# A hybrid linear-attention and pooling layer: a norm product in its own tile, context gates by pairs of heads, key weights in other tiles

## The chip, the cores and the metric

One core of a Trainium2 chip runs the whole program. The metric is device time in microseconds (us) of one execution. The engines are named as the profile names them: PE (TensorE, matrix products), DVE (VectorE), ACT (ScalarE), POOL (GpSimd) and SP (SyncE, which issues the transfers).

## The reference

One layer of a diffusion backbone works on 1024 latent tokens and 256 context tokens of width 1024. All is float32. Cut to what matters here:

```python
h  = rmsnorm(x, norm_g) * (1 + scale) + shift            # context and latent alike
q, k, v, la_f, la_b, zA, uB, zB, gA, gB = mixer_inputs(h, w_in, ...)
gk = lowrank @ w_up + b                                  # rank 16, per direction
la = log_sigmoid(gk) / 16                                # log decay, 4 heads x 128 keys
...
S_t = diag(a_t) S_(t-1) + k_t v_t^T ;  o_t = q_t S_t      # both directions
# the latent scan starts from the context's final state of the same direction
...
merged = sigmoid(gA) * yA + sigmoid(gB) * yB
x_new  = x + gate_x * (merged @ w_out)
out    = x_new * rsqrt(mean(x_new ** 2) + eps) * final_norm_g
```

Of the context, only the final state of each head and direction is needed: keys times the decay that is still to come, transposed, times values.

## The kernel before, in words

Every float32 operand of a product is split in two: ACT copies it to a rounded `hi` tile and DVE subtracts that to get a `lo` tile (`split`, L84). A product is then three matmuls: hi by hi, hi by lo, lo by hi. Helpers record nearly all instructions, so most rows carry a helper's line: L64 is any ACT operation, L67 a DVE operation of two tensors, L71 and L72 a DVE operation with a scalar, L79 a matmul, L330 the scan.

Tiles come from pools by tag. Each tag has a fixed number of buffers (L38): `wr` 2 (raw weights as loaded), `wh` and `wl` 4 each (their split), `s2` 8, `on` 1, `bx` 1, `z` 2. A new tile of a tag waits until the oldest one's last reader is done. The eight PSUM banks of 128x512 are tags too (L40): `pj` 3, `sc` 2, `o`, `st` and `tr` one each. The order of the instructions on each engine is not the order of the program's text: a scheduler places them, and weight loads with their splits are placed ahead (`tc.high_priority` in `wslot`, L259) once the first context head is done (L697).

The program has these stages around the change:

1. Norms and modulation, and the first projections with all the input weights that come first.
2. **Context gates** (`ctx_gates`, L336). For each of four heads and two directions, `gate_in` (L323) makes a 128x256 result with two matmuls of 64 rows (the low-rank factor by the up-projection's hi and lo). One head's two directions share the bank of tag `o`. ACT takes the absolute value out of the bank (with the bias) and DVE the minimum with zero. When all heads are there, ACT does Exp, then Ln, each over two heads at a time, in the tiles `z`; DVE subtracts and scans (L330) along the tokens. The rest of the decays is computed from the scans.
3. **Latent gates of head 0** (`gates`, L462): the same in banks `sc`, `sc`, `o` and `tr`, with 128x512 results, and Exp and Ln over one `bx` tile of 128x2048.
4. **Context states** (`ctx_state`, called in the loop at L698): for heads 1 to 3 the key weights (`weights_k`, L383, through `wslot`: one load into `wr`, two pairs of `wh`/`wl`) and value weights (`weights_v`: two loads, four pairs). `ctx_k` makes 24 matmuls into a `pj` bank, `ctx_v` two times 24. `ctx_state` multiplies the keys by two exponentials, transposes them on PE into bank `tr`, copies them to the one `on` tile on ACT, and multiplies them with the values into bank `st` (8 matmuls).
5. The latent attention of four heads, the pooling branch, the branches' projections.
6. **The output product**, in seven block products (`out_product`, L1227) whose results are added to the residual tiles `y` (these have the tile names `h`, `kt`, `sw`, `v`, `S`) by DVE (`add_y`, L1198). Products 5 and 6 complete eight token tiles of 128 rows, four each: 12 matmuls per tile into one bank. `finish` (L1209) then squares the completed half on ACT (with the row sum), multiplies it by the final gain `fg` on DVE in place (both in `square`, L1201), makes the scale of the row (a DVE operation on 128x1, a POOL power), scales one half on DVE and the other on ACT, and stores both halves (256 KB each). The other half of a tile has been squared and multiplied before (`first_done`).

Of the kernel before, what the change touches and what calls it, by code (L numbers as in the profile page):

```python
# [10 lines left out]
F32R = mybir.dt.float32r  # L11
# [4 lines left out]
P = 128  # L16
# [27 lines left out]
def hybrid_kernel(ctx: ExitStack, tc: tile.TileContext, x, ctx_in, rows, w_mod, b_gate_row,  # L44
# [213 lines left out]

    def wslot(src, shape, col_scale=None):  # L259

# [3 lines left out]
        with tc.high_priority() if ahead[0] else nullcontext():  # L264
# [4 lines left out]
            for k0 in range(0, nk, per):  # L269
                kn = min(per, nk - k0)  # L270
                hi, lo = T("wh", [P, kn, n], F32R), T("wl", [P, kn, n], F32R)
                split(hi, lo, raw[:, k0:k0 + kn, :])
                parts += [(hi[:, i, :], lo[:, i, :]) for i in range(kn)]
        return parts

    def wcols(w, c0, n=P):
        return w[:, c0:c0 + n].rearrange("(k p) n -> p k n", p=P)
# [58 lines left out]
    def ctx_gates():  # L336
# [3 lines left out]
        for h in range(NH):  # L340
            pt = PT("o")
            for d in range(2):
                pd = pt[:, d * LC:(d + 1) * LC]
                bcol = gate_in(pd, h, d, 0, LC)
                act(e[h // 2][:, h % 2, d, :], pd, AF.Abs, bias=bcol)
                ts(xm[h // 2][:, h % 2, d, :], pd, bcol, ALU.add, 0.0, ALU.min)
# [35 lines left out]

    def weights_k(h):  # L383
        return wslot(wcols(w_in, O_K + h * P), [P, KT, P])

# [312 lines left out]
    for h in range(1, NH):  # L698
        ctx_state(h, ctx_k(weights_k(h)), ctx_v(weights_v(h)))
    o_dram = [dr.tile([KT, P, 256], F32, name=f"o{h}") for h in range(NH)]  # L700
# [508 lines left out]
    def finish(t, dh):  # L1209
        square(t, dh)  # L1210
        ts(yst[:, t, 1:2], yss[:, t, dh:dh + 1], 1.0 / D, ALU.mult, yst[:, t, 0:1], ALU.add)
        nc.gpsimd.tensor_tensor(out=yst[:, t, 2:3], in0=yst[:, t, 1:2], in1=mhalf, op=ALU.pow)
        for dh in range(2):
            if dh:
                act(y[t][dh], y[t][dh], scale=yst[:, t, 2:3])
            else:
                ts(y[t][dh], y[t][dh], yst[:, t, 2:3], ALU.mult)
            load(out[t * P:(t + 1) * P, dh * HALF:(dh + 1) * HALF], y[t][dh])

# [35 lines left out]
    for t in range(CPH):  # L1255
        add_y(CPH + t, 1, sums[t])
        first_done(CPH + t, 1)
    out_product(5, others, True)
    for t in range(CPH):
        add_y(CPH + t, 0, others[t])  # L1260
        finish(CPH + t, 0)
    out_product(6, sums, True)
    for t in range(CPH):
        add_y(t, 1, sums[t])
        finish(t, 1)

# [64 lines left out]
```

## Time and profile before

| | us |
|---|---|
| median of 3 runs (range) | 1116.48 (1116.02 to 1117.79) |
| the profiled execution's own time | 1116.68 |
| its span in the profile | 1114.9 |
| PE busy | 1080.9 (97%) |
| DVE busy | 819.7 (74%) |
| ACT busy | 511.4 (46%) |
| granted clock of PE, mean | 0.996 |

The span counts from the first to the last instruction of the profile; the execution's own time is 1.8 us longer. Busy time is what instructions took, so that a share near 100% over the whole program says which engine sets the time on the mean, and the stages where the share is lower must be looked at one by one. The granted clock is a share of the full 2.4 GHz.

### The profile page before, as it was taken

How to read it: one execution, taken by the hardware profiler on the slowest of the kernel's cores; microseconds unless marked ns; L12 is line 12 of the kernel's file. 1: busy time of each engine (PE TensorE's matmuls, PEld its weight loads, DVE VectorE, ACT ScalarE, POOL GpSimd, SP SyncE). 2: the span in 40 equal slices, each digit the busy share in tenths (PEclk: the TensorE clock that was granted, in tenths of full speed). 3: DMA queues.
4: the chain of work that ended last, by engine and by line, in shares of the span. 5: the costliest groups of instructions: out<-in, count | busy, mean ns of one | idle time of the engine just before them, and what ended most of it. 6: DMA issues, size and time to landing. Idle time of an engine off the chain costs nothing.

```text
span 1114.9 us, 16534 instructions
## 1 busy us (share of the span) xinstructions
PE 1080.9 (97%) x6073; PEld 872.6 (78%) x6073; DVE 819.7 (74%) x1518; ACT 511.4 (46%) x982; POOL 24.9 (2%) x50
## 2 busy tenths in 40 slices
PE   7999899999999999999999999999999999999995
PEld 1497887797887888888888888788887788888884
DVE  4775768487586685989989987877778786557854
ACT  4875864644644744543334343333436423124433
POOL 0000000100100000000000000000000000000001
PEclk9999999999999999999999999999999999999998
DMA  9920240310310311114331884865628658645424
GB/s 332 299 58 20 68 141 21 84 50 20 95 39 20 96 39 39 48 48 129 125 115 51 290 273 134 258 208 206 195 96 290 203 186 287 232 132 181 149 77 151
DMA packets 124470, 152.85 MB, mean 137 GB/s; under 512 B 9515, under 2 KB 77413, under 8 KB 124262
## 3 DMA queue, kind: packets, MB, share of 16 engines
q1 hardware_dynamic: 124390, 151.80, 42.8%
q8 instruction: 48, 0.79, 0.3%
q14 instruction: 32, 0.26, 0.1%
HBM read 107.72 MB, written 39.85 MB: 132 GB/s over the span
## 4 chain that ended last, share of the span: by engine, by line
PE 70%; DMA 10%; DVE 8%; ACT 6%; issue 3%; POOL 1%; SPq 0%; POOLq 0%; ACTq 0%; DVEq 0%
PE ppj L79 47%; PE psc L79 14%; PE pst L79 3%; PE po L79 2%; DMA wr<-w_in 2%; DMA h<-w_mod 2%; DVE s L67 2%; DVE wl L67 1%; PE ptr L79 1%; DMA wo_T<-t 1%; DVE wr L67 1%; ACT on L64 1%; ACT A L64 1%; ACT wh L64 1%; DMA S<-ctx 1%
## 5 line engine op out<-in xcount | busy, mean ns | idle before, releaser
L79 PE MATMUL ppj<-h,wh 128*128 128x512 f32 x730 | 238.8, 400 | 0.0
L79 PEld LDWEIGHTS ppj<-h,wh 128*128 128x128 f32 x730 | 136.1, 188 | 32.7 <-issue 3.0
L64 ACT ACTIVATE wh<-wr 128x512 fp32r<-128x512 f32 x162 | 99.6, 626 | 117.6 <-DVE wr L67 39.0
L79 PE MATMUL ppj<-h,wl 128*128 128x512 f32 x365 | 143.3, 393 | 0.0
L67 DVE TENSOR_TENSOR wl<-wr,wh 128x512 fp32r<-128x512 f32 x162 | 110.1, 688 | 35.6 <-ACT wh L64 34.7
L79 PE MATMUL ppj<-wh,h 128*128 128x256 f32 (+1 forms) x518 | 96.2, 285 | 0.0
L79 PEld LDWEIGHTS ppj<-wh,h 128*128 128x128 f32 x518 | 81.4, 192 | 1.4 <-issue 0.7
L79 PEld LDWEIGHTS ppj<-h,wl 128*128 128x128 f32 x365 | 68.6, 188 | 14.6 <-issue 1.0
L79 PE MATMUL ppj<-wl,h 128*128 128x256 f32 x259 | 73.7, 285 | 0.0
L64 ACT ACTIVATE s<-s 128x512 f32<-128x512 f32 x60 | 36.9, 628 | 30.9 <-DVE s L67 29.1
L79 PEld LDWEIGHTS ppj<-wl,h 128*128 128x128 f32 x259 | 49.7, 192 | 0.4
L75 DVE SCALAR_TENSOR_TENSOR S<-S,dec,pst 128x256 f32<-128x256 f32 x56 | 26.9, 480 | 29.4 <-PE pst L79 28.6
L64 ACT ACTIVATE s<-qk 128x256 f32<-128x256 f32 x56 | 23.5, 426 | 47.1 <-DVE qk L67 46.9
L67 DVE TENSOR_TENSOR s<-s,ppj 128x512 f32<-128x512 f32 x60 | 40.5, 681 | 1.4 <-issue 1.2
L79 PE MATMUL ppj<-S,wh 128*128 128x512 f32 (+1 forms) x124 | 38.5, 376 | 1.3 <-ACT wh L64 1.3
L79 PE MATMUL psc<-h,wh 128*128 128x512 f32 x126 | 39.2, 392 | 0.0
L64 ACT ACTIVATE qk<-wr 128x512 fp32r<-128x512 f32 x30 | 18.5, 627 | 44.2 <-DVE wr L67 26.9
L67 DVE TENSOR_TENSOR s<-s,bx 128x256 f32<-128x256 f32 (+1 forms) x64 | 30.5, 486 | 7.5 <-ACT bx L64 7.5
L79 PEld LDWEIGHTS psc<-z,s 128*64 128x64 f32 x768 | 25.0, 136 | 10.5 <-issue 9.0
L79 PE MATMUL ppj<-v,wh 128*128 128x512 f32 (+1 forms) x108 | 32.9, 367 | 0.0
L67 DVE TENSOR_TENSOR on<-wr,wr 128x512 f32<-128x512 f32 x21 | 14.5, 691 | 24.6 <-DMA wr<-w_in 18.3
L79 PE MATMUL pst<-v,kt 128*128 128x256 f32 x112 | 31.2, 395 | 1.2 <-DVE S L75 1.2
(666 smaller groups left out, 2487.8 us busy)
## 6 DMA issues: line engine op xcount, KB each, us to landing
wr<-w_in SPq DMA_DIRECT2D x65, 512.0 KB, 4.1
h<-w_mod SPq DMA_DIRECT2D x48, 256.0 KB, 5.6
qk<-sg SPq DMA_DIRECT2D x32, 256.0 KB, 5.3
sg<-s SPq DMA_DIRECT2D x28, 256.0 KB, 2.5
sw<-qk SPq DMA_DIRECT2D x64, 64.0 KB, 2.0
gb_T<-qk SPq DMA_DIRECT2D x16, 256.0 KB, 2.8
t<-w_out SPq DMA_DIRECT2D x4, 1024.0 KB, 5.5
qk<-o SPq DMA_DIRECT2D x16, 256.0 KB, 4.5
```

The costliest lines, as they stand in the source:

```text
L64: return nc.scalar.activation(out, in_, func, **kw)
L67: return nc.vector.tensor_tensor(out=out, in0=a, in1=b, op=op)
L75: return nc.vector.scalar_tensor_tensor(out=out, in0=a, scalar=s, in1=b, op0=op0, op1=op1)
L79: return nc.tensor.matmul(out, lhsT=lhsT, rhs=rhs, start=start, stop=stop, skip_group_check=joined)
```

## The change: three edits and the order they give

`wslot` takes the tags of the split tiles as an argument, and the key weights of head 1, the first of the loop at L698, use `s2` for both. `ctx_gates` takes two banks for each pair of heads, `o` for the one direction and `tr` for the other, and issues the pair's 16 matmuls before the reads. `finish` no longer calls `square`: the product with the gain goes to a new `s2` tile, the scaling and the stores are in a function `store`, and the end loops call it one tile later in the program's text. In the changed file the lines after L344 stand 2 further down, those at the end up to 8.

```diff
--- before.py
+++ after.py
@@ -256,7 +256,7 @@
 
     ahead = [False]
 
-    def wslot(src, shape, col_scale=None):
+    def wslot(src, shape, col_scale=None, tags=("wh", "wl")):
 
         _, nk, n = shape
         per = HALF // n
@@ -268,7 +268,7 @@
                 tt(raw, raw, col_scale.rearrange("p (k n) -> p k n", k=1).to_broadcast(shape), ALU.mult)
             for k0 in range(0, nk, per):
                 kn = min(per, nk - k0)
-                hi, lo = T("wh", [P, kn, n], F32R), T("wl", [P, kn, n], F32R)
+                hi, lo = [T(t, [P, kn, n], F32R) for t in tags]
                 split(hi, lo, raw[:, k0:k0 + kn, :])
                 parts += [(hi[:, i, :], lo[:, i, :]) for i in range(kn)]
         return parts
@@ -338,10 +338,12 @@
         xm = T("bx", [P, 2, 2, 2, LC])
         xm = [xm[:, i] for i in range(2)]
         for h in range(NH):
-            pt = PT("o")
+            if h % 2 == 0:
+                pts = [PT(t) for t in ("o", "tr")]
+                at = lambda h, d: pts[d][:, h % 2 * LC:(h % 2 + 1) * LC]
+                bcols = [[gate_in(at(i, d), i, d, 0, LC) for i in (h, h + 1)] for d in range(2)]
             for d in range(2):
-                pd = pt[:, d * LC:(d + 1) * LC]
-                bcol = gate_in(pd, h, d, 0, LC)
+                pd, bcol = at(h, d), bcols[d][h % 2]
                 act(e[h // 2][:, h % 2, d, :], pd, AF.Abs, bias=bcol)
                 ts(xm[h // 2][:, h % 2, d, :], pd, bcol, ALU.add, 0.0, ALU.min)
         for t in e:
@@ -380,8 +382,8 @@
             act(vc[:, t, :], proj_n(wv, hcH, hcL, slice(t * P, (t + 1) * P))[:, :256])
         return vc
 
-    def weights_k(h):
-        return wslot(wcols(w_in, O_K + h * P), [P, KT, P])
+    def weights_k(h, **kw):
+        return wslot(wcols(w_in, O_K + h * P), [P, KT, P], **kw)
 
     def weights_v(h):
         return wquad(w_in, O_V + h * 256)
@@ -696,7 +698,7 @@
     ctx_state(0, kc, ctx_v(wv))
     ahead[0] = True
     for h in range(1, NH):
-        ctx_state(h, ctx_k(weights_k(h)), ctx_v(weights_v(h)))
+        ctx_state(h, ctx_k(weights_k(h, tags=("s2", "s2") if h == 1 else ("wh", "wl"))), ctx_v(weights_v(h)))
     o_dram = [dr.tile([KT, P, 256], F32, name=f"o{h}") for h in range(NH)]
     ga_dram = [dr.tile([P, L], F32, name=f"ga{i}") for i in range(2 * NH)]
 
@@ -1207,15 +1209,19 @@
         ts(yst[:, t, 0:1], yss[:, t, dh:dh + 1], 1.0 / D, ALU.mult, EPS, ALU.add)
 
     def finish(t, dh):
-        square(t, dh)
+
+        act(T("on", [P, HALF]), y[t][dh], AF.Square, accum_out=yss[:, t, dh:dh + 1])
+        scaled = T("s2", [P, HALF])
+        tt(scaled, y[t][dh], half(fg, dh), ALU.mult)
         ts(yst[:, t, 1:2], yss[:, t, dh:dh + 1], 1.0 / D, ALU.mult, yst[:, t, 0:1], ALU.add)
         nc.gpsimd.tensor_tensor(out=yst[:, t, 2:3], in0=yst[:, t, 1:2], in1=mhalf, op=ALU.pow)
-        for dh in range(2):
-            if dh:
-                act(y[t][dh], y[t][dh], scale=yst[:, t, 2:3])
-            else:
-                ts(y[t][dh], y[t][dh], yst[:, t, 2:3], ALU.mult)
-            load(out[t * P:(t + 1) * P, dh * HALF:(dh + 1) * HALF], y[t][dh])
+
+        def store():
+            act(scaled, scaled, scale=yst[:, t, 2:3])
+            ts(y[t][1 - dh], y[t][1 - dh], yst[:, t, 2:3], ALU.mult)
+            for h_, v in ((1 - dh, y[t][1 - dh]), (dh, scaled)):
+                load(out[t * P:(t + 1) * P, h_ * HALF:(h_ + 1) * HALF], v)
+        return store
 
     def out_part(pt, i, t, g, joined):
         (a_hi, a_lo), (x_hi, x_lo) = m_ops[g][OUT_PRODUCTS[i][0]], w_ops[OUT_PRODUCTS[i][1]][g]
@@ -1255,14 +1261,16 @@
     for t in range(CPH):
         add_y(CPH + t, 1, sums[t])
         first_done(CPH + t, 1)
-    out_product(5, others, True)
-    for t in range(CPH):
-        add_y(CPH + t, 0, others[t])
-        finish(CPH + t, 0)
-    out_product(6, sums, True)
-    for t in range(CPH):
-        add_y(t, 1, sums[t])
-        finish(t, 1)
+    store = None
+    for i, t0, dh, banks in ((5, CPH, 0, others), (6, 0, 1, sums)):
+        out_product(i, banks, True)
+        for t in range(CPH):
+            add_y(t0 + t, dh, banks[t])
+            after = finish(t0 + t, dh)
+            if store:
+                store()
+            store = after
+    store()
 
 
 def shape_constants():
```

The scheduler makes a new order out of this. Outside of the stages 2 to 4 (and a few instructions of head 0's attention that were placed among them) and of the last two output products, no engine's order changes. Three places:

PE, at the end of the context gates. `po_1030` is the gate bank of a context head, `psc`, `po_1127` and `ptr_1134` the banks of the latent gates of head 0, `ppj_1181` the first product of context values:

```order
 L79 MATMUL psc_1111<-lr_1007,lr_436 128x512
-L79 MATMUL po_1030<-lr_833,lr_436 128x256
-L79 MATMUL po_1030<-lr_833,lr_437 128x256
 L79 MATMUL psc_1111<-lr_1007,lr_437 128x512
 L79 MATMUL psc_1118<-lr_1007,lr_436 128x512
 L79 MATMUL psc_1118<-lr_1007,lr_437 128x512
+L79 MATMUL ppj_1181<-wh_534,h_835 128x256
+L79 MATMUL ppj_1181<-wl_535,h_835 128x256
+L79 MATMUL po_1127<-lr_782,lr_436 128x512
+L79 MATMUL po_1127<-lr_782,lr_437 128x512
 L79 MATMUL ptr_1134<-lr_782,lr_436 128x512
 L79 MATMUL ptr_1134<-lr_782,lr_437 128x512
```

Before, the context's gate matmuls stand in eight separate pairs, some of them within the value products, and those of `po_1127` after them. Now they stand in three groups (8, 4 and 4 matmuls) ahead of the latent gates, and all latent gates stand ahead of the third value matmul.

ACT, up to `on_1349`, the copy of the transposed keys of context head 0, for which PE's state product (`pst`) waits. Before (`wh_1360` and `wh_1364` are the splits of head 1's key weights, `bx` the latent gates' Ln, `S_1286` the context values):

```order
L64 ACTIVATE wh_1360<-wr_1358 128x512
L64 ACTIVATE wh_1364<-wr_1358 128x512
L64 ACTIVATE wh_1397<-wr_1395 128x512
L64 ACTIVATE wh_1401<-wr_1395 128x512
L64 ACT_TABLE_LOAD
L64 ACTIVATE bx_1108<-bx_1108 128x2048
L64 ACTIVATE S_1286<-ppj_1313 128x256
L64 ACTIVATE on_1349<-ptr_1344 128x512
```

After (the Ln on `bx` and the splits of head 1's key weights are done ahead of these rows; `kt_1468` is head 1's exponential, `s_243` and `s_244` the latent decays):

```order
L64 ACTIVATE v_1233<-ppj_1260 128x256
L64 ACTIVATE wh_1397<-wr_1395 128x512
L64 ACTIVATE S_1286<-ppj_1287 128x256
L64 ACTIVATE wh_1401<-wr_1395 128x512
L64 ACT_TABLE_LOAD
L64 ACTIVATE kt_1468<-kt_1468 128x256
L64 ACTIVATE wh_1407<-wr_1405 128x512
L64 ACTIVATE wh_1411<-wr_1405 128x512
L64 ACTIVATE s_243_1109<-s_243_1109 128x512
L64 ACTIVATE s_244_1110<-s_244_1110 128x512
L64 ACTIVATE S_1286<-ppj_1313 128x256
L64 ACTIVATE on_1349<-ptr_1344 128x512
```

The copy to `on_1349` has moved behind splits of later weights and behind exponentials of the latent decays. On PE, the state product that waits for `on_1349` stood behind all 24 key products of head 1 and six value products; now it stands behind 21 of the key products, and three key products and 24 value products come after it.

DVE, at the end: the last tile of product 5 (`h_9847`) and the first add of product 6 (`kt_9766`). Before:

```order
L67 TENSOR_TENSOR h_9847<-h_9847,ptr_10086 128x512
L67 TENSOR_TENSOR h_9847<-h_9847,z_9899 128x512
L72 TENSOR_SCALAR yst<-yss,yst 128x1
L71 TENSOR_SCALAR h_9847<-h_9847,yst 128x512
L67 TENSOR_TENSOR kt_9766<-kt_9766,psc_9903 128x512
```

After:

```order
L67 TENSOR_TENSOR h_9847<-h_9847,ptr_10086 128x512
L67 TENSOR_TENSOR s_1897_10325<-h_9847,z_9899 128x512
L72 TENSOR_SCALAR yst<-yss,yst 128x1
L71 TENSOR_SCALAR h_9848<-h_9848,yst 128x512
L67 TENSOR_TENSOR kt_9766<-kt_9766,psc_9903 128x512
```

The product goes to `s_1897`, and DVE now scales the tile's other half (`h_9848`). That scaling still stands ahead of the next tile's add: in the queue it is not a tile later.

## Rows read from the trace of the kernel before

**Rows 1.** Part 1 of the page: busy us, share of the span, instructions, by engine.
```profile
PE 1080.9 (97%) x6073; PEld 872.6 (78%) x6073; DVE 819.7 (74%) x1518; ACT 511.4 (46%) x982; POOL 24.9 (2%) x50
```
**Rows 2.** Windows over the middle: window, us, busy by engine (instructions), PE's granted clock, DMA.
```profile
90.00:115.30 25.30, 24.02 (x146) 19.12 (x146) 15.64 (x34) 17.83 (x27) 0.20 (x2) 1.00 0.07 16
115.30:133.40 18.10, 14.85 (x110) 13.58 (x110) 12.65 (x28) 16.46 (x28) 0.00 (x0) 1.00 0.20 59
133.40:142.00 8.60, 8.31 (x63) 7.74 (x62) 8.59 (x35) 6.48 (x13) 0.00 (x0) 1.00 0.61 177
```
**Rows 3.** Timeline of PE: start, us, instruction, count, [idle before <- what ended it].
```profile
104.74 0.50 PE L79 MATMUL po<-lr,lr 64*128 64x256 f32 x2 [0.94 <-DVE bx L72]
...
123.00 0.39 PE L79 MATMUL ppj<-S,wh 128*128 128x256 f32 x1 [1.34 <-ACT wh L64]
...
128.54 1.99 PE L79 MATMUL pst<-S,on 128*128 128x256 f32 x8 [1.22 <-ACT on L64]
```
**Rows 4.** Timeline of DVE and ACT over one tile of output product 5.
```profile
1087.39 0.68 DVE L67 TENSOR_TENSOR S<-S,ppj 128x512 f32<-128x512 f32 x1
1088.16 0.63 ACT L64 ACTIVATE on<-S 128x512 f32<-128x512 f32 x1 [0.45 <-DVE S L67]
1088.92 0.69 DVE L67 TENSOR_TENSOR S<-S,z 128x512 f32<-128x512 f32 x1 [0.85 <-ACT on L64]
1089.53 0.21 DVE L72 TENSOR_SCALAR yst<-yss,yst 128x1 f32<-128x1 f32 x1
...
1090.41 0.49 DVE L71 TENSOR_SCALAR S<-S,yst 128x512 f32<-128x512 f32 x1 [0.68 <-POOL yst L1212]
1090.81 0.68 DVE L67 TENSOR_TENSOR h<-h,ppj 128x512 f32<-128x512 f32 x1
```
**Rows 5.** Timeline of the tail: first and last add and scale (DVE), two banks' last matmuls (PE).
```profile
1083.96 0.68 DVE L67 TENSOR_TENSOR v<-v,ppj 128x512 f32<-128x512 f32 x1
...
1100.03 0.40 PE L79 MATMUL po<-wh,S 128*128 128x512 f32 x1
...
1102.83 0.40 PE L79 MATMUL pst<-wh,S 128*128 128x512 f32 x1
...
1107.31 0.68 DVE L67 TENSOR_TENSOR h<-h,pst 128x512 f32<-128x512 f32 x1
...
1110.32 0.48 DVE L71 TENSOR_SCALAR h<-h,yst 128x512 f32<-128x512 f32 x1 [0.66 <-POOL yst L1212]
```
**Rows 6.** Timeline of PE among the context gates: eight projection matmuls, then a gate pair.
```profile
93.04 2.09 PE L79 MATMUL ppj<-h,s 128*128 128x512 f32 x8
95.06 0.50 PE L79 MATMUL po<-lr,lr 64*128 64x256 f32 x2
```
**Rows 7.** Timeline of ACT and DVE over the gates, splits and copies in the middle.
```profile
97.88 1.28 ACT L64 ACT_TABLE_LOAD   x1
99.17 1.06 ACT L64 ACTIVATE z<-z 128x1024 f32<-128x1024 f32 x1
...
112.45 1.29 DVE L67 TENSOR_TENSOR bx<-bx,z 128x512 f32<-128x512 f32 x2 [1.28 <-ACT z L64]
115.69 0.83 DVE L330 TENSOR_TENSOR_SCAN z<-cst,z,bx 128x128 f32<-128x128 f32 x2
116.56 0.86 ACT L64 ACTIVATE bx<-psc,cols 128x256 f32<-128x256 f32 x2 [1.83 <-DVE z L330]
120.52 1.91 ACT L64 ACTIVATE bx<-bx 128x2048 f32<-128x2048 f32 x1
122.32 2.19 ACT L64 ACTIVATE wh<-wr 128x512 fp32r<-128x512 f32 x4
127.90 0.59 ACT L64 ACTIVATE on<-ptr 128x512 f32<-128x512 f32 x1
```
**Rows 8.** Windows around the last matmul (columns as in rows 2).
```profile
1103.00:1105.00 2.00, 0.22 (x1) 0.00 (x0) 1.08 (x2) 1.05 (x2) 0.47 (x1) 1.00 0.39 146
1105.00:1106.00 1.00, 0.00 (x0) 0.00 (x0) 0.57 (x1) 0.40 (x2) 0.00 (x0) 0.74 1.04 385
```

## The prediction

> **What bounds the kernel now.** I read the page's part 1 first, to see which engine could set the time. PE is busy for 1080.9 us of the 1114.9 us span [rows 1], so over most of the program only less PE work or less PE waiting can help, and what DVE and ACT do beside it is free. All of PE's idle time is 34 us, so I looked next for where it lies near the edits. Windows over the gates and context states show it: PE is idle 25.30 - 24.02 = 1.28 us in 90 to 115.3, 18.10 - 14.85 = 3.25 us in 115.3 to 133.4 and 8.60 - 8.31 = 0.29 us in 133.4 to 142, all at a granted clock of 1.00 [rows 2]. PE's timeline gives the waits by name: 0.94 us of a context gate pair for DVE's read of the bank, 1.34 us of head 1's first key product for its split weights, 1.22 us of the state product for ACT's copy `on` [rows 3]. Last I read the end on DVE and ACT, because after the last matmul PE cannot be the bound: one tile's add, square, product, scale and next add show who waits for whom [rows 4].
>
> **The tail.** One tile costs DVE 1090.81 - 1087.39 = 3.42 us from add to add [rows 4]. PE makes a bank in 1102.83 - 1100.03 = 2.80 us [rows 5], so there DVE is the bound and runs late. 0.85 us of the cycle is the product's wait for ACT's square: it overwrites the tile that ACT reads [rows 4]. In its own tile the product needs the add alone, so it runs beside the square, and the 128x1 operation, which needs the square's row sum, comes where the product stood: at 1088.92 for 1089.53, 0.61 us sooner [rows 4]. All behind it moves along, since the queue still has the scaling ahead of the next add: "one tile later" does not come about on DVE, and the 0.68 us wait for POOL stays. The cycle becomes 3.42 - 0.61 = 2.81 us, call it 2.82, just above PE's 2.80. From the first add at 1083.96, seven cycles end at 1103.70, against 1107.31 in the trace [rows 5]: 3.61 us. PE is no closer bound: its last result is there at 1103.23. One add that the old order had put ahead of a scaling (the new has not) is within both figures. From the last add to the last scale it was 1110.32 - 1107.31 = 3.01 us [rows 5] and is 0.61 less: together **4.2 us**. The stores move forward with the scalings, two per tile as before. I price a longer queue of stores at nothing: the two are issued each 2.82 us instead of 3.42, and the DMA share is 0.39 in one window of the tail and 1.04 in the next [rows 8], so transfers come in bursts with room between. If that cover fails, a part of the 4.2 is given back at the last store.
>
> **The context gates.** A context gate pair takes 0.50 us of PE's row and breaks a run of projection products whose eight take 2.09 us [rows 6]. Within one run the products start 0.232 us apart, so eight would need 1.85 us; I read the rest, about 0.17 us, as what a change from 128-row to 64-row matmuls and back costs. Five breaks fewer (three groups for eight): 0.85 us. The waits of 1.28 us [rows 2] stand mainly before such pairs, because one bank must be read by ACT and DVE before the next head enters it [rows 3]; with two banks for two heads the reads of four results run behind four products. About 0.3 of it remains, where the latent gates need the banks `o` and `tr` back. Bounds: 0.85 and 0.85 + 0.95 = 1.8 us; I take **1.2**, nearer to the lower, since the third group waits for the second's reads. So what ended at 115.3 [rows 2] ends about 114.1.
>
> **The middle, walked along the new order.** What comes early there is the ACT chain. Its last Abs of the context, which followed a gate pair at 104.74 [rows 3], now ends at about 101, then a table load of 1.28 and an Exp of 1.06 [rows 7], each twice with Exp and Ln: 106. DVE's subtracts started at 112.45 [rows 7], now at about 106, and the scans, whose last two end at 116.52 [rows 7], end about 110.3. Behind them ACT reads the latent banks (116.56 before [rows 7]), which takes 4.9 us with Abs of other halves between, does Exp to 117.1, a split, a table load and the Ln of 1.91 us [rows 7], to 120.75. Head 1's key weights need no `wh`/`wl` now, so the 2.19 us of four splits that stood behind that Ln [rows 7] no longer hold PE: head 1's first key product starts about 121.1, when the copy that frees its bank, first in the queue behind the Ln, is over, instead of 123.00 [rows 3].
>
> Then the order takes it back. `on_1349`, the copy for the state product, stands behind eleven ACT instructions (three copies of values, four splits, a table load, three exponentials); from 120.75 with the durations of like rows they end about 126.7, and the copy of 0.59 us [rows 7] at 127.3, against 128.49 before. PE has done its 21 key products by 121.1 + 21 × 0.12 = 123.7 and **waits some 3.5 us**, where it waited 1.22. The state product then takes its 1.65 us, three key and 24 value products 27 × 0.12 = 3.2: the next value product can start at about 132.4 where it started at 133.50. That is 1.1 us, the 1.2 that came in from the gates: so in 115 to 133 the change itself is worth **0**. Behind, a transposition's wait of 0.29 us goes [rows 2]: **0.3**. From 142 us to the tail no order changes and PE is never idle for long, so what is won here reaches the end.
>
> **The clock.** A wait of 3.5 us has a price of its own. The granted clock was 1.00 to 1105, 0.74 on average in the next us [rows 8], so it fell to its lower level (1.2 of 2.4 GHz) about 2.3 us after the last matmul had ended at 1103.23 [rows 5]. The new wait is longer. No row shows how a return looks, so I bound it: nothing, if the clock holds; and all of the work from the state product to 132.4 at half speed, 1.65 + 3.2 = 4.85 us more, call it 4.95 with the pieces between. I take **1.2 us lost**: half speed over a stretch as long as the one that the clock took to fall, 2.3 us, costs about half of it again; that is the nearest row. The Trainium skill, "TensorE: Matmul & The Clock Gate", section "HAM oscillation — how this bites in real kernels", says that a wait between groups of matmuls can send the engine back to the lower clock, that the next group then starts cold, and that activity lifts it again. By that rule the time is the 1112.0 below; by a clock that holds, 1110.8; the rows before the tail, all at 1.00, hold no wait as long and decide neither.
>
> **The sum.** 4.2 + 1.2 + 0 + 0.3 - 1.2 = 4.5 us off the profiled execution's own 1116.68 us: 1112.2. That execution was 0.2 above the median of the three, 1116.48, so I forecast **1112.0 us**.
>
> **Rivals.**
> *The clock holds over the wait.* For it: PE's short idle times in the middle left it at 1.00 [rows 2]. Against: this one is longer than the 2.3 us after which it fell at the end. Then 1.2 more is won: 1110.8. Chance 0.28.
> *The tail does not get shorter.* If what ended the product's wait is not the overwriting but something else on ACT (the row sum is needed anyhow, and ACT has its own scaling per tile), or the stores end it, the 4.2 goes and the middle's 0.3 remains: about 1116.2, no change. For it: two stores of 256 KB per tile come a fifth more densely. Against: the page names ACT's square as the releaser in every tile [rows 4]. Chance 0.07.
> *Slower: the ACT chain does not come early.* If scans still end at 116.4, because an ACT or DVE instruction of the new order that I walked past waits for something late (a weight load, the `s2` tiles that the splits now need), then everything behind them comes 6.1 us later than I walked and the copy `on_1349` ends at 133.4 instead of 128.5. PE stands for about 9 us, and the clock's price is at its upper bound: 1112.0 + 6.1 + 4.95 - 1.2 = 1121.9. With that clock price it turns slower once the scans end after about 111.1, with 1.2 only after about 114.8. For it: eleven instructions are queued ahead of the one that PE needs. Against: Abs, Exp, Ln and scans depend only on banks that are ready by 102. Chance 0.04.
> *The stores are not a tile later.* The order shows so, and the forecast has that in.
>
> **How the numbers follow.** The forecast has 0.53. The remaining 0.08 I give to a gain in the gates at its upper bound with a copy that comes earlier than walked: 1109. The range goes from 1109.6, a gates' gain of 1.8 with the clock at nothing, to 1114.3, half of the clock's upper price beyond the one taken. It takes in the first rival. 0.2% of this kernel is 2.2 us, about what a measurement can tell from no change. Faster by more than that is all below 1114.25: the forecast but for its dearest clock, the first rival and the larger gain, 0.87. Within it lie the tail rival and a bit of the forecast: 0.09. Slower: 0.04.
>
> **What would show it.** In the changed profile: add to add 2.8 us in the tail, no wait of the product for ACT, and the last add about 3.6 us nearer to the first; context gates in three groups, what ended at 115.3 over about 114.1; no wait of head 1's first key product for a split; a wait of some 3.5 us before the state product with ACT's `on` as releaser; a granted clock under 1.00 in 125 to 135. I am wrong if the tail's cycle stays at 3.4, if the state product's wait is under 2 or over 6 us, or if the copy comes after 128.5.

## The result: 7.0 us less, where 4.5 were forecast

| | before | after |
|---|---|---|
| median, first series (executions; range) | 1117.13 us (4; 1116.02 to 1117.81) | 1109.2 us (4; 1107.51 to 1111.62) |
| median, second series | 1117.65 us (11; 1115.52 to 1121.51) | 1110.98 us (6; 1109.14 to 1112.9) |
| ratio, first series | | 0.9937, 95% interval 0.9925 to 0.995 |
| ratio, second series | | 0.9938, 95% interval 0.992 to 0.9956 |
| the profiled execution's own time | 1116.68 us | 1108.54 us |

The change is faster by 0.63%, 7.0 us (5.6 to 8.4; the medians of the first series lie 7.9 apart, within that interval), where 4.5 were forecast. The median of 1109.2 lies 0.4 us below the range's low end of 1109.6, that of the second series, 1110.98, inside the range. The direction and the two places were right. One term, the context gates, was too small.

Part 1 of the changed kernel's page answers to [rows 1]: PE works 2.5 us less in a span that is 8.2 us shorter.

```profile
PE 1078.4 (97%) x6073; PEld 873.5 (79%) x6073; DVE 819.9 (74%) x1518; ACT 511.5 (46%) x982; POOL 24.8 (2%) x50
```

The windows of [rows 2], in the changed kernel (window, us, then busy by engine, PE's granted clock, DMA share, GB/s):

```profile
90.00:115.30 25.30, 24.63 (x169) 21.23 (x169) 20.60 (x47) 22.73 (x36) 0.20 (x2) 1.00 0.06 14
115.30:133.40 18.10, 14.01 (x97) 12.94 (x97) 12.20 (x42) 13.43 (x24) 0.00 (x0) 0.91 0.30 88
133.40:142.00 8.60, 8.60 (x72) 7.99 (x70) 4.92 (x9) 7.27 (x15) 0.00 (x0) 1.00 0.43 120
```

In the first window PE gets through 169 matmuls where it had 146. In the second it is idle for 4.09 us, more than the 3.25 before, and the clock is no longer 1.00. What PE waits for there, on its timeline, with the product that follows:

```profile
100.09 0.76 PE L79 MATMUL po<-lr,lr 64*128 64x512 f32 x2 [0.67 <-DVE bx L72]
...
119.77 0.39 PE L79 MATMUL ppj<-S,s 128*128 128x256 f32 x1 [0.97 <-ACT v L64]
...
125.64 3.50 PE L79 MATMUL pst<-S,on 128*128 128x256 f32 x8 [3.12 <-ACT on L64]
```

Against [rows 3], head 1's first key product no longer waits for a split and begins at 119.77 instead of 123.00. The state product waits 3.12 us instead of 1.22 and then takes 3.50 us for what took 1.99. Windows from the last key product on show why:

```profile
122.50:125.00 2.50, 0.02 (x1) 0.00 (x0) 1.84 (x6) 2.50 (x6) 0.00 (x0) 1.00 0.72 204
125.00:126.00 1.00, 0.36 (x1) 0.36 (x2) 1.00 (x5) 0.90 (x3) 0.00 (x0) 0.65 0.29 59
126.00:128.50 2.50, 2.50 (x7) 1.96 (x7) 2.50 (x15) 0.00 (x0) 0.00 (x0) 0.50 0.59 192
128.50:129.50 1.00, 1.00 (x8) 0.92 (x7) 1.00 (x6) 0.32 (x1) 0.00 (x0) 0.89 0.00 0
```

PE does nothing from 122.5 to 125.6, and the clock falls to its lower level (0.50, 1.2 GHz) near the wait's end and stays there until the state product is nearly over.

One tile of the tail, the same as in [rows 4]:

```profile
1082.91 0.68 DVE L67 TENSOR_TENSOR S<-S,ppj 128x512 f32<-128x512 f32 x1
...
1083.62 0.69 DVE L67 TENSOR_TENSOR s<-S,z 128x512 f32<-128x512 f32 x1
1083.68 0.64 ACT L64 ACTIVATE on<-S 128x512 f32<-128x512 f32 x1 [0.45 <-DVE S L67]
1084.22 0.19 ACT L64 ACTIVATION_READ_ACCUMULATOR on<-S 128x1 f32 x1
1084.44 0.21 DVE L72 TENSOR_SCALAR yst<-yss,yst 128x1 f32<-128x1 f32 x1
...
1085.33 0.49 DVE L71 TENSOR_SCALAR S<-S,yst 128x512 f32<-128x512 f32 x1 [0.67 <-POOL yst L1217]
1085.73 0.68 DVE L67 TENSOR_TENSOR h<-h,ppj 128x512 f32<-128x512 f32 x1
```

The product runs beside the square, and the 128x1 operation waits only for the row sum. From add to add it is 2.82 us instead of 3.42. The first add, the last and the last scale, against [rows 5]:

```profile
1080.09 0.68 DVE L67 TENSOR_TENSOR v<-v,ppj 128x512 f32<-128x512 f32 x1
...
1099.78 0.68 DVE L67 TENSOR_TENSOR h<-h,pst 128x512 f32<-128x512 f32 x1
...
1102.19 0.49 DVE L71 TENSOR_SCALAR h<-h,yst 128x512 f32<-128x512 f32 x1 [0.66 <-POOL yst L1217]
```

**Where the 8.14 us between the two profiled executions went.** PE has the same 6073 matmuls in both and, outside the stages touched, in the same order, so the start of the matmul with one number in that order can be compared. The 370th, ahead of the first edit, is 0.26 us earlier (nothing differs until there: chance). From it to the 1201st, at 190 us, 2.05 us are won; to the 5001st, at 852 us before, 0.23; to the 5301st 1.34; the rest, 4.26 us, in the tail. Of the 1.34, 1.25 are two waits in the pooling and branch stages that no edit touches, first before, then after:

```profile
858.64 0.97 PE L79 MATMUL ppj<-h,qk 128*128 128x512 f32 x3 [1.50 <-DVE s L67]
...
873.26 0.73 PE L79 MATMUL pst<-z,wh 128*128 128x512 f32 x2 [1.37 <-ACT wh L64]
```

```profile
855.21 0.95 PE L79 MATMUL ppj<-h,qk 128*128 128x512 f32 x3 [0.60 <-DVE s L67]
...
869.47 0.72 PE L79 MATMUL pst<-z,wh 128*128 128x512 f32 x2 [1.02 <-ACT wh L64]
```

Open after this: whether these waits belong to the change, what the gates won and why, which edit the long wait belongs to, what the clock costs, and whether taking that wait away wins its time. "Won by 190 us" below is always from the 370th to the 1201st matmul, against the profile of before.

### The profile page after: what moved, and what is told of

The parts are those of the page before. It is cut to its first block, busy times and chain, and to the rows that moved or that the text cites. A ratio compares the mean times of both kernels' runs of the same rounds, so it can differ in the third digit from the quotient of the medians.

```text
span 1106.7 us, 16531 instructions
## 1 busy us (share of the span) xinstructions
PE 1078.4 (97%) x6073; PEld 873.5 (79%) x6073; DVE 819.9 (74%) x1518; ACT 511.5 (46%) x982; POOL 24.8 (2%) x50
## 4 chain that ended last, share of the span: by engine, by line
PE 82%; ACT 6%; DMA 5%; DVE 4%; issue 2%; POOL 1%; SPq 0%; POOLq 0%; ACTq 0%; DVEq 0%
PE ppj L79 54%; PE psc L79 18%; PE pst L79 4%; PE po L79 2%; PE ptr L79 2%; DMA h<-w_mod 1%; DMA wr<-w_in 1%; ACT on L64 1%; ACT A L64 1%; POOL r L623 1%; ACT z L64 1%; PE psc L177 1%; ACT sw L64 1%; PE ptr L369 1%; ACT L64 1%
## 5 line engine op out<-in xcount | busy, mean ns | idle before, releaser
L67 DVE TENSOR_TENSOR s<-s,psc 128x512 f32<-128x512 f32 x43 | 29.1, 681 | 3.4 <-PE psc L79 3.4
L67 DVE TENSOR_TENSOR z<-z,bx 128x512 f32<-128x512 f32 x48 | 30.9, 686 | 0.0
```

What stands on the lines that cost most here:

```text
L67: return nc.vector.tensor_tensor(out=out, in0=a, in1=b, op=op)
```

## The experiments

### One part at a time

**The tail's edit alone**: `finish` and the end loops of the change, the rest as before.

> The tail's edit alone. The theory (the product no longer waits for ACT's square, so a tile's cycle on DVE falls from 3.42 to 2.82 us, and the last tile's chain is 0.61 us shorter): 4.2 us faster than before, last add 7 x 2.82 = 19.7 us behind the first, all else as before. The rival (the 1.3 us that the changed kernel's profile won between 640 and 875 us belong to this edit's moved tiles): 5.5 us faster, with the waits at 857 and 871 us shorter here too.

1113.72 us against 1117.41, ratio 0.9959 (0.9943 to 0.9974): 4.6 us. First add at 1087.49, last at 1107.18, 19.69 us; last scale 2.41 us behind it. The two waits were longer than in any other profile:

```profile
860.22 0.96 PE L79 MATMUL ppj<-h,qk 128*128 128x512 f32 x3 [2.64 <-DVE s L67]
...
875.55 0.81 PE L79 MATMUL pst<-z,wh 128*128 128x512 f32 x2 [2.12 <-ACT wh L64]
```

From the first add to the last scale that is 22.10 us instead of 26.36 [rows 5]. So the tail's 4.2 us stand, and the rival falls: its waits came out longer, not shorter. With the middle's order just as before, PE was 0.43 us later by 190 us than in the profile of before: a first figure for the scatter of this measure.

**The gates alone**: `ctx_gates` of the change.

> The context gates by pairs alone; key weights of head 1 in wh and wl as before. Theory A (the three edits add up, the key weights help head 1's first key product to start early): less won than gates and keys together, under 2 us. Theory B (with the key weights in other tiles ACT gets the splits of later weights ahead of the copy that the state product waits for, so that edit costs): by the new order the state product stands behind 9 key products, ACT's copy for it ends at about 123.1 us, PE waits 1.2 us and not 3.1, the clock stays at 1.00, and the product that began at 133.5 us before begins at about 129.8: 3.7 us faster than before.

1115.37 us, ratio 0.9983 (0.9974 to 0.9992): 1.9 us, and 2.07 us won by 190 us. That is under the 2 us of theory A, but not less than with the keys (below). Theory B is wrong: without the key weights' edit the long wait is there too, one step earlier. The key product waits 2.87 us for its split, and the clock falls behind that:

```profile
121.89 0.51 PE L79 MATMUL ppj<-S,wh 128*128 128x256 f32 x1 [2.87 <-ACT wh L64]
```

```profile
122.00:125.00 3.00, 3.00 (x11) 2.60 (x12) 3.00 (x7) 2.46 (x6) 0.00 (x0) 0.50 0.18 26
```

**The key weights alone**: the tags in `wslot` and the loop.

> Head 1's key weights in s2 alone. Theory A: a gain of up to 1.3 us, the wait of head 1's first key product for its split (1.34 us before) goes and nothing takes its place. Theory B: the splits of the value weights come ahead of ACT's copy for the state product, which ends at about 129.6 us and not 128.5; PE waits some 3.4 us for it, long enough for the clock to fall to half: between 0 and 1 us slower, within 0.2% of before.

1118.65 us, ratio 1.0009 (0.9999 to 1.0018): 1.0 us slower, the size that B gave, but the interval reaches no difference. PE was 2.36 us later by 190 us. B's wait did not come where it was forecast: the key products wait for nothing, a value product then waits 2.68 us for ACT's copy of a value tile, which frees its bank, and the state product behind it does not wait but takes 3.62 us, at the lower clock:

```profile
128.09 0.58 PE L79 MATMUL ppj<-wh,S 128*128 128x256 f32 x1 [2.68 <-ACT S L64]
```

**Gates and keys, without the tail**:

> The change without its tail edit. If the parts of the two profiles add up: the middle's 2.0 us faster than before, with the state product's wait of 3.1 us and the half clock behind it as in the changed kernel. The rival (the shorter waits at 857 and 871 us come from the middle's shift and not from one execution to the next): 3.4 us faster, with both waits short as in the changed kernel.

1116.32 us, ratio 0.9989 (0.9975 to 1.0004): 1.2 us, and 1.69 us won by 190 us, with the wait (3.09 us) and the half clock. The waits at 858 and 873 us were 1.48 and 1.48 us, as before the change. Gates alone won 2.07 and with the keys 1.69, a difference within the scatter of 0.43: the keys' edit moves the wait from the key product to the state product, and no gain of it shows.

### What the gates won

**Two banks, but head by head**: each head's four matmuls, then its reads.

```diff
-            if h % 2 == 0:
-                pts = [PT(t) for t in ("o", "tr")]
-                at = lambda h, d: pts[d][:, h % 2 * LC:(h % 2 + 1) * LC]
-                bcols = [[gate_in(at(i, d), i, d, 0, LC) for i in (h, h + 1)] for d in range(2)]
+            pts = [PT(t)[:, :LC] for t in ("o", "tr")]
+            bcols = [gate_in(pts[d], h, d, 0, LC) for d in range(2)]
             for d in range(2):
-                pd, bcol = at(h, d), bcols[d][h % 2]
+                pd, bcol = pts[d], bcols[d]
```

> The change with the two banks kept for the two directions, but head by head: four groups of two and two gate matmuls, each head read before the next may enter. The context's value products begin at 115.4 us before and 112.5 us in the changed kernel. If fewer breaks of PE's run win it (theory: a break costs PE some 0.5 us, and the two directions' matmuls, on the two halves of PE's rows, run at the same time where they stand together): they begin in between, at 113 to 114.5 us. If the reads of the banks win it (rival, PE waits for no read any more): no gain over before, since each head again waits for the last one's reads, 115 us or later.

From the start of the projection run ahead of the gates (82.22 us before, 81.97 after, 81.88 here) to the context's first value product it is 33.14 us before (to 115.36), 30.55 after (to 112.52) and 31.23 here (to 113.11). So the change wins **2.59 us** at this place, and 1.91 of them come without pairs of heads: the first product began within the theory's 113 to 114.5 us. The rival falls as the whole cause, but a part is its: PE's waits for reads of the banks are 1.28 us in this stretch before, 0.67 in the change and 0.58 here. Total time 1111.38 us, ratio 0.9949 (0.993 to 0.9967). Behind the gates this run's order is another one (the transposition and the state product stand behind most of head 1's 48 value products), so its time does not tell what the pairs of heads are worth; its longest wait there was 1.63 us, the clock stayed at 1.00, and by 190 us it had won 2.75 us:

```profile
101.54 0.73 PE L79 MATMUL po<-lr,lr 64*128 64x512 f32 x2 [0.58 <-DVE bx L72]
...
124.87 0.50 PE L79 MATMUL ppj<-S,s 128*128 128x256 f32 x2 [1.63 <-DVE s L67]
```

What the matmuls themselves do stands in the changed kernel's timeline of PE:

```profile
90.12 0.38 PE L79 MATMUL po<-lr,lr 64*128 64x256 f32 x1
90.13 0.38 PE L79 MATMUL ptr<-lr,lr 64*128 64x256 f32 x1
90.34 0.28 PE L79 MATMUL po<-lr,lr 64*128 64x256 f32 x1
90.36 0.28 PE L79 MATMUL ptr<-lr,lr 64*128 64x256 f32 x1
...
90.80 3.24 PE L79 MATMUL ppj<-h,s 128*128 128x512 f32 x13
93.97 0.73 PE L79 MATMUL po<-lr,lr 64*128 64x256 f32 x4
94.63 0.74 PE L79 MATMUL ppj<-h,s 128*128 128x512 f32 x2
95.29 0.74 PE L79 MATMUL ptr<-lr,lr 64*128 64x256 f32 x4
95.96 0.97 PE L79 MATMUL ppj<-h,s 128*128 128x512 f32 x3
```

The queue has four `po` and then four `ptr`, but they start in twos, 0.01 us apart: the two directions use the two halves of PE's 128 rows, and in two banks they run at the same time. Eight take 0.68 us (90.12 to 90.80), four of one direction 0.66 (93.97 to 94.63) and 0.67 (95.29 to 95.96): 2.01 us for all sixteen. Before, a pair alone takes 0.43 us (95.06 to the next product at 95.49); seven pairs stand alone and one among the latent gates, 3.16 us in all. So the 2.59 us are three parts: 1.15 in the gate matmuls' own time, 0.61 in waits (1.28 - 0.67), and the remaining 0.83 in the products around them, whose run is broken less often. The Trainium skill, "TensorE: Matmul & The Clock Gate", section "Part 3: Packing small matmuls — row/col tiling", says that matmuls with few rows run concurrently where they lie in different row groups; the trace agrees.

### The wait of 3.1 us and the clock

**The wait filled**: 22 matmuls that nothing needs, between the key products and the state product; the real product overwrites their bank.

```diff
+                for _ in range(22):
+                    tc.keep_in_program_order(mm(pt[:, :256], hcH[0][:, :P], hcL[0], True, True))
```

> The changed kernel with 22 more matmuls (128x256, the context's first rows, into the state's bank, where the real product overwrites them) placed between head 1's key products and the state product, so that PE works through the wait of 3.1 us and nothing else changes. If the half clock behind that wait is what it costs (theory): the granted clock stays at 1.00, the eight rows of the state product take 1.65 us and not 3.15, and the transposition behind the next 48 value products comes 1.5 us earlier than in the changed kernel. If the state product is slow for itself, by its new operand or bank (rival): it takes 3.1 us at any clock shown, and nothing is won.

```profile
122.99 2.77 PE L79 MATMUL pst<-v,S 128*128 128x256 f32 x22
```

```profile
125.90 1.99 PE L79 MATMUL pst<-S,on 128*128 128x256 f32 x8
```

The clock stayed at 1.00 and the state product took 1.99 us: the half clock is all that made it 3.50, a price of 1.5 us, and the rival falls. The transposition behind the value products came at 133.42 instead of 135.01. By the time it won nothing (1112.73 us, ratio 0.9957, 0.9943 to 0.9972): the state product and what follows it were recorded in another place, the order behind 133 us differs, and by 190 us PE was where it is in before, after new waits of 0.86 and 1.43 us and with 22 more matmuls done.

**The copies early**: transposition and copies for head 0's state at high priority, the state product at lower.

```diff
-            act(vc[:, t, :], proj_n(wv, hcH, hcL, slice(t * P, (t + 1) * P))[:, :256])
+            pv = proj_n(wv, hcH, hcL, slice(t * P, (t + 1) * P))[:, :256]
+            with tc.high_priority() if not ahead[0] else nullcontext():
+                act(vc[:, t, :], pv)
...
-        kT = transpose_k([kk[:, d, t * P:(t + 1) * P] for d in range(2) for t in range(2)], "on")
+        with tc.high_priority() if h == 0 else nullcontext():
+            kT = transpose_k([kk[:, d, t * P:(t + 1) * P] for d in range(2) for t in range(2)], "on")
...
+        with tc.high_priority(offset=-40) if h == 0 else nullcontext():
```

> The changed kernel with ACT's copies for head 0's state (the transposed keys and both value copies) at high priority and the state product at lower priority: by the order that this gives, the copy of the keys stands ahead of the Ln and the state product behind 24 key products and 14 value products. Theory (the gain of the gates is held back only by where the state product stands and by the clock behind its wait): no wait over 1.5 us on PE between 115 and 133 us, a granted clock of 1.00 throughout, head 1's second value product begins at about 128.4 us where the changed kernel has 132.2: 3.8 us faster than the changed kernel, some 9 to 10 us faster than before. Rival (ACT's chain of Exp, Ln and splits sets the end of this stretch, and PE only waits elsewhere, for the split of the value weights): the wait moves to the value products and under 1.5 us are won.

1110.9 us, ratio 0.9939 (0.9924 to 0.9954): the changed kernel's time, and 2.19 us won by 190 us. The waits behind 116 us went, but the transposition that I had put ahead now waited for its bank, and the clock fell behind this wait of 2 us:

```profile
115.95 0.63 PE L369 MATMUL ptr<-cst,kt 128*128 128x128 f32 x4 [1.99 <-DVE s L72]
```

```profile
117.00:121.00 4.00, 4.00 (x23) 4.00 (x22) 0.99 (x3) 3.86 (x4) 0.00 (x0) 0.57 0.47 131
```

**The state product later**: nothing but its place on PE, behind 24 key products and 33 value products (its four matmuls, two rows each in the profile, then stand one value product apart).

```diff
-        for d in range(2):
-            for c in range(2):
-                mm(pt[:, d * 256:(d + 1) * 256], kT[:, d * 2 + c, :], vc[:, c, :], c == 0, c == 1)
+        with tc.high_priority(offset=-60) if h == 0 else nullcontext():
+            for d in range(2):
+                for c in range(2):
+                    mm(pt[:, d * 256:(d + 1) * 256], kT[:, d * 2 + c, :], vc[:, c, :], c == 0, c == 1)
```

> The changed kernel with one thing moved: head 0's state product has lower priority, so on PE it stands behind all 24 key products of head 1, its first 24 value products and part of the second 24, and nothing waits for ACT's copy of the keys; ACT's order up to that copy is the same. Theory (only the place of the state product holds back what the gates won, by its wait of 3.1 us and, in some executions, by the clock's fall behind it): no wait of more than 1 us on PE between 120 and 131 us, a granted clock of 1.00 there, and the transposition behind the 48 value products begins at about 130.5 us where the changed kernel has 135.0, or 133.5 in an execution whose clock held: 3 to 4.5 us faster than the changed kernel, 1105 to 1106 us. Rival (the value products wait for their splits by as much): the wait moves to a product of the value weights, and under 1 us is won.

1110.31 us, ratio 0.9927 (0.9914 to 0.9941): 8.2 us, not to be told from the change's 7.0. Up to 130 us it did what the theory said: no wait over 0.97 us, the clock at 1.00, the transposition at 130.07 instead of 135.01. Then it was given back, to head 2's weights and to the next head's state product, which waits for its own copy:

```profile
131.59 0.39 PE L79 MATMUL ppj<-S,wl 128*128 128x256 f32 x1 [0.68 <-DVE wl L67]
...
136.22 1.99 PE L79 MATMUL pst<-S,on 128*128 128x256 f32 x8 [2.13 <-ACT on L64]
```

So both theories were half right: the place of the one product held PE back, but behind it PE waits for ACT's copy for the next head. By 190 us this run had won 3.26 us.

**The same with the scaling held back** (next section's edit):

> The same, and in the tail the scaling on DVE held behind the next tile's add and product, as in the run before. Theory: as state_later, and 0.3 us less from the first add of the tail to the last; the two can't be told apart by their times, only by the tail's rows.

1110.01 us, ratio 0.993 (0.9914 to 0.9946). The adds of the tail were 19.30 us from first to last. What it showed besides is the clock. The same wait stands at the same place as in the run before, but here the product behind it took 2.79 us, at a clock of 0.65 on average:

```profile
136.25 2.79 PE L79 MATMUL pst<-S,on 128*128 128x256 f32 x8 [2.13 <-ACT on L64]
```

```profile
136.20:140.00 3.80, 3.75 (x14) 3.27 (x15) 1.90 (x3) 2.29 (x8) 0.00 (x0) 0.65 0.52 142
```

By 190 us this run had won 1.83 us, where the one before had won 3.26.

### The tail

**The own tile alone**: the product in its own tile, stores in place and halves shared as before.

> The change, but with the stores where they were before in the text and the scaling shared as before (lower half on DVE, upper on ACT): of the tail's edit only the product's own tile is left. Theory (the own tile is all that wins): 2.82 us from add to add as in the changed kernel, the time the changed kernel's. Rival (scaling the other half on DVE, or the later stores, win a part): over 2.9 us from add to add.

1110.72 us, ratio 0.9938 (0.9922 to 0.9954), the change's own. Adds from 1081.68 to 1101.39, 2.82 us each: the own tile does it all.

**The stores really a tile later**:

```diff
-            ts(y[t][1 - dh], y[t][1 - dh], yst[:, t, 2:3], ALU.mult)
+            tc.keep_in_program_order(ts(y[t][1 - dh], y[t][1 - dh], yst[:, t, 2:3], ALU.mult))
```

> The change, with the scaling of a tile on DVE held behind the next tile's add and product, so that the stores really come a tile later. Theory (with 2.82 us DVE is hardly behind PE's 2.80 per bank, so there is little left): add to add 2.80 us, set by PE, the last add some 0.3 us nearer to the first, and the end within 0.5 us of the changed kernel's, since the last but one tile's two stores now come close to the last's. Rival (the tail is still DVE's): over 1 us faster.

1109.38 us, ratio 0.9924 (0.9904 to 0.9944). Now the adds wait for PE:

```profile
1096.67 0.69 DVE L67 TENSOR_TENSOR h<-h,po 128x512 f32<-128x512 f32 x1 [0.64 <-PE po L79]
1099.47 0.69 DVE L67 TENSOR_TENSOR h<-h,pst 128x512 f32<-128x512 f32 x1 [0.65 <-PE pst L79]
```

2.80 us from add to add and 19.41 from first to last, 0.28 less than in the change: the theory. Most of it goes again at the end, where two scalings now stand behind the last product: from the first add to the last scale it is 22.00 us against the change's 22.10. The order of the middle is the change's, and so is the wait, but in this execution the clock held (compare the 3.50 us above):

```profile
125.86 1.99 PE L79 MATMUL pst<-S,on 128*128 128x256 f32 x8 [3.10 <-ACT on L64]
```

```profile
126.00:128.50 2.50, 2.50 (x15) 2.29 (x16) 2.50 (x15) 0.72 (x3) 0.00 (x0) 1.00 0.71 206
```

### The change once more

> The changed kernel once more, for more executions and a second profile. Theory (the tail's 4.2 us are in every execution, the middle's part is 2.1 us where the clock falls behind the state product's wait of 3.1 us and 3.2 where it holds, and the 1.3 us that the first profile of the change won at 857 and 871 us are chance): 6.3 to 7.4 us faster than before in the same call, the wait of 3.1 us there again, and the state product's eight rows at 3.2 to 3.5 us or at 2.0, as the clock falls or holds. Rival (the waits at 857 and 871 us are shorter by the change): both short again, and 7.6 us or more.

Ratio 0.9938 again, 6.9 us. The wait was 3.10 us and the state product took 3.48 us. The waits at 856 and 870 us were 1.13 and 1.29 us, 2.42 together, against 1.62 in the change's first profile, 2.87 before and 4.76 with the tail alone. They vary from one execution to the next, as the theory had it. But the nine profiles that hold all three edits, varied or not, have 1.62 to 3.27, and the four of one part or two 2.96 to 4.76. Those four were all measured on one chip, and none of the nine was measured in that series, so whether the edits together shorten these waits (means of 2.46 and 3.87 us, with 2.87 before) is open.

Of the five profiles with the change's middle and its wait of 3.1 us (the change twice, gates and keys, the own tile, the stores later) the clock fell in four and held in one. By 190 us the four had won 1.59 to 2.05 us and the one 3.21. That is as much as the state product's later place won (3.26, with the clock held, and 1.83 where it fell behind the next wait): in these single profiles it is the clock that sets the kernels apart by 190 us, and moving the product shows no gain of its own.

## Why the prediction was right where it was, and which step failed

| step | forecast | measured |
|---|---|---|
| tail: seven cycles | 3.61 us (3.42 to 2.82 each) | 23.35 - 19.69 = 3.66 us |
| tail: last add to last scale | 0.61 us | 3.01 - 2.41 = 0.60 us |
| context gates: products around | 0.85 us | 0.83 us |
| context gates: waits | 0.35 us, bounds 0 and 0.95 | 0.61 us |
| context gates: the gate matmuls' own time | nothing | 1.15 us |
| context gates, together | 1.2 us, bounds 0.85 and 1.8 | 2.59 us |
| wait of the state product | about 3.5 us | 3.12 us |
| price of the clock behind it | -1.2 us, bounds 0 and -4.95 | -1.5 us where it falls, 0 where it holds |
| the rest up to 190 us | 0.3 us | 2.05 - 2.59 + 1.5 = 1.0 us |
| sum up to 190 us | 0.3 us | 2.05 us (1.59 in the second profile) |

The tail and the part up to 190 us make 4.26 + 2.05 = 6.3 of the 7.0 us; the other 0.7 is within the interval, and no run ties it to an edit.

**The tail** came as reckoned, term by term, and for the reason given. That the deferral of the stores does not come about on DVE was right too, and so was its worth: when it does come about, it is 0.28 us at the last add and 0.10 at the last scale. The rival of a tail that does not get shorter is out.

**The gates** are the step that failed: "Five breaks fewer (three groups for eight): 0.85 us", with bounds of 0.85 and 1.8. That price came out right in sum for what it covers (0.83 us), and the waits came out nearer to their upper bound. What was left out is the pair's own time, put at nothing: I priced a break by what the products around it lose, 0.17 us, and took the pair's own time as there either way; but the pair alone takes 0.43 us, more pairs behind one another take less each, and two directions in two banks run at once. That is 1.15 us. Both could be read from the trace of before: the next product after the pair of [rows 6] starts 0.43 us behind it and not 0.50, and a latent and a context gate matmul start there 0.04 us apart (at 98.74 and 98.78 us).

**The walk along ACT's order** found the right events: no wait for a split, the state product behind ACT's copy, a wait that grows from 1.22 to 3.12 us, half the clock behind it. All came 1.3 to 1.7 us earlier than walked, about what the gates had won beyond the forecast: the first key product at 119.77 and not 121.1, the end of `on` at 125.59 and not 127.3. One reading was wrong and cost nothing: the row at 120.52 of [rows 7] is the Exp, and the four splits stood behind it and ahead of the Ln, which starts at 125.82 and takes 1.92 us. The rest up to 190 us was 1.0 and not 0.3: waits there grew by 0.5 us in all, and the products between them stand 1.5 us closer together; why, no run shows.

**The clock**: its price was nearly right, but as a mean, and partly by luck. In one execution it is 1.5 us or nothing, so that the forecast and the rival of a clock that holds are both true, in four profiles of five and in one. The 1.2 came from the 2.3 us that the clock took to fall at the program's end; what it cost was half of the 3.1 us that PE worked at the lower clock (125.64 to about 128.7, by the windows' means), and no row of before shows that stretch. What the Trainium skill, "TensorE: Matmul & The Clock Gate", section "HAM oscillation — how this bites in real kernels", says is borne out where the clock fell: the group behind the wait starts at the lower clock (3.50 us for eight rows and not 1.99), and by 129 us the engine is back at 1.00 while it works. The wait alone does not settle whether it falls: the same wait left the clock at 1.00 once.

**The slower rival**, an ACT chain that does not come early, is out: reads of the latent gates begin at 109.02 instead of 116.56 [rows 7].

```profile
109.02 0.86 ACT L64 ACTIVATE bx<-psc,cols 128x256 f32<-128x256 f32 x2 [1.53 <-DVE z L330]
```

**The range** does not follow from its own words: 1112.0 less 0.6 for a gates' gain of 1.8 and 1.2 for a clock at nothing is 1110.2, not 1109.6, and half of the clock's upper price gives 1113.9 or 1114.5, not 1114.3.

## What to carry to other kernels

Where one operation waits for another engine only because both use one tile, give it its own: the win is what each round gets shorter times the number of rounds (here 0.6 us of a wait of 0.85, since the row sum is still waited for), as long as the next bound (here PE, 2.80 us against 2.82) lies below. A gain ahead of a chain on another engine can stop at the first instruction that the chain feeds, and moving that instruction need not free it: it won 4.9 us at that place against the change's first profile, 1.3 of them the clock's (133.73 us where it held), and nothing by 190 us against the profile whose clock held (3.26 and 3.21), since the chain is late for the next one as well. When matmuls of few rows stand between others, price their own time and not only the change of kind, and ask which of them could run side by side.

## What the runs showed of the hardware

The clock behind a wait of PE is a matter of the execution: a wait of 3.10 us left it at 1.00 in one profile, and one of 3.09 to 3.12 us brought it to 0.50 in four; one of 2.13 us, in two kernels with the same order there, once left it and once cost 0.8 us in the product behind it alone. Matmuls on the two halves of PE's rows, queued four and four into two banks, ran in twos, 0.01 us apart. And two waits at 855 to 876 us, in a stage with the same order in all kernels, took between 1.62 and 4.76 us together, 1.62 and 2.42 in two profiles of one kernel, so that differences of an edit's size arise far from the edit.
